# Seven products instead of eight for one more row pair in three stages of a two-layer decoder kernel

## The chip, the cores and the metric

The kernel runs on one core of one Trainium2 chip. The metric is the device time of one execution in microseconds (us). Three runs of the kernel before took 2260.9, 2261.01 and 2262.21 us, median 2261.01.

## The reference

The reference is a trunk of two decoder layers in float32 over 256 tokens of width 2048. Layer 0 mixes tokens with a gated linear recurrence (HGRN2, 12 heads of 128), layer 1 with gated linear attention (GLA, 4 heads, key width 192, value width 384). In both, one input projection also feeds a cross-attention of four heads into 256 memory tokens, and a SwiGLU feed-forward network follows. Cut to what the change touches:

```
# layer 0
q, f, i, g, xq = split(hn @ w_in)          # MIX_WIDTH = 1536 columns each, xq 512
f = sigmoid(f);  k = 1 - f;  q = silu(q)   # with a learned lower bound for f
o = chunked_linear_attention(q, k, i, log f)
y = rmsnorm_per_head(o) * silu(g)
# layer 1
q, k, v, g, gk_low, xq = split(hn @ w_in)  # q and k 768 columns, v and g 1536
# both
h = h + concat(y, memory_attention(xq)) @ w_out
```

`hn` is the normalized `h`; the kernel multiplies the row scales in after the projection.

## The kernel before

**Products.** All float32 products run on TensorE as three matmuls each: both factors are split into a high part (rounded to fp32r by ScalarE) and a low part (the rest, by VectorE), and a product is high x high, high x low and low x high. Activations are the stationary factor (128 rows of `h` turned, times 128 tokens), weights the moving one (512 columns, 384 in layer 1).

**Row pairs.** `project_two` (line 528 on) computes two column blocks of a weight matrix at once, for two tiles of 128 tokens, over the 2048 rows taken as eight pairs of 128-row slices. A pair is then a 2x2-by-2x2 block product. In a plan string with one letter per pair, `-` does it plainly, in eight products (24 matmuls, two `split` calls), and `S` in seven (21 matmuls) by a Strassen-like scheme (`seven`): it needs sums of the weight blocks (`raw` tiles, more subtractions on VectorE and four `split` calls) and sums of the activation blocks, which are made once per layer and kept (`Pair.more`, four extra factors in two parts). The letters S take pairs 0, 1, 2 ... in this order; the letters `-` take the pairs from the count of S on. Where `fed` holds (layer 0), one of the weight sums of an S is made by the load itself: SP loads one block, POOL's queue adds a second block onto it by an accumulating DMA.

**Buffers.** Three `raw` tiles hold loaded weights, six `parts` tiles the split ones; a plain pair takes two `parts`, an S pair three and one of two small `part` tiles. The memory keys and values that the attention reads also lie in `parts` buffers while it runs. The tag `tq` has eight buffers: a `more` takes one, a quad of turned mixer outputs (`y_0` to `y_3`) two.

**Layer 0, first mixer.** `h_quad` turns the normalized input (names `hx`); pairs below `SEVEN` get a `more`. Then come the xq projection (`hx`) and three groups of four heads. Each group g has two stages of `project_two`: forget gate and query (`hf0`, `hf1`, `hf2` in the trace), then value and output gate (`hv0`, `hv1`, `hv2`; with plan `----SSS-`, in the last group `----SS--`). After the last group comes the output projection: `wo` (512 columns, over the four y quads in the order 3, 0, 1, 2), then `wo0p`, and so on.

**Layer 1, second mixer.** Two pairs of heads; each has a key and query stage (`gk0`, `gk1`) and two value and gate stages (`gg00` to `gg11`, plan `-----SS-`). Here `fed` is off, and VectorE makes the sum.

**The queue of pieces.** The attention-like work between projections is cut into pieces and queued by `later`; `step` takes the next piece off the queue and issues it. A stage calls `step` twice in each plain pair (once for each 128-row slice), and once more where over `MANY` = 12 pieces wait; an S pair calls it only where over 12 wait. After each f/q stage 18 pieces are queued: two empty ones, `turn_f`, `turn_q`, two empty ones, and the twelve of `gated_scores` (`even_diagonal`, `pairs`, `level(2)` to `level(6)`, `across`, with empty ones between). After each value stage come `read` (readout, norm and gate) and `turn_y` (turning the result into a y quad) with empty ones before and between. In `wo` a step comes at five places, and ahead of the last y quad `y_done` issues all that is left (`flush`). The empty pieces space dependent pieces apart.

**Order.** Instructions are issued in the order of the program, but a list scheduler in the compiler puts a later instruction of an engine ahead of one that it expects not to be ready. Each engine then runs its list in order.

Of the kernel before, what the change touches and what calls it, by code (L numbers as in the profile page):

```python
# [13 lines left out]
AF = mybir.ActivationFunctionType  # L14
# [9 lines left out]
MIX = 1536  # L24
# [4 lines left out]
DK = 192  # L29
# [11 lines left out]
def trunk_kernel(ctx: ExitStack, tc: tile.TileContext, x, mem, norm_mix, norm_ffn, norm_mem,  # L41
# [210 lines left out]
    def later(*pieces):  # L252
        pending.extend(pieces)
# [391 lines left out]
        return ps  # L645


    SEVEN = 3
    MANY = 12


# [101 lines left out]
    for l in range(2):  # L753
# [6 lines left out]
        if l == 0:  # L760
# [4 lines left out]
            hq, ss, first_turns = {}, new_ss("ss_x"), []  # L765
# [207 lines left out]
    def hgrn_group(w, g, hq, r, yq):  # L973

        st = {}

        def stages(plan, *what):
            dst = []

            def give():  # L980
                for c0, name, func in what:
                    tag, bufs = ("stg", 2) if name in "fq" else (name, 1)
                    dst.append(work.tile([P, NT, 512], F32, tag=tag, name=f"{name}s{g}", bufs=bufs))
                return [lambda t, d=d: d[:, t, :] for d in dst]

            (ca, na, fa), (cb, nb, fb) = what
            project_two(hq["pairs"], plan, w, ca + 512 * g, cb + 512 * g, 512, f"h{na}{g}", give)
            for d, (c0, name, func) in zip(dst, what):
                for t in range(NT):
                    ac.activation(out=d[:, t, :], in_=d[:, t, :], func=func, scale=r[:, t:t + 1])  # L990
            return dst

        def turn_f():
            F = work.tile([P, NT, 4, P], F32, tag="F", name=f"F{g}")
            K = st["K"] = work.tile([P, NT, 4, P], F32, tag="K", name=f"K{g}")
            for j in range(2):
                tp = transposes([lambda t, c=2 * j + i: fs[:, t, c * P:(c + 1) * P] for i in range(2)], f"tf{g}{j}")
                for i in range(2):
                    c = 2 * j + i
                    ve.tensor_scalar(out=F[:, :, c, :], in0=tp[:, i * T:(i + 1) * T].rearrange("p (t c) -> p t c", c=P),  # L1000
                                            scalar1=oml[:, 4 * g + c:4 * g + c + 1],
                                            scalar2=lb[:, 4 * g + c:4 * g + c + 1], op0=ALU.mult, op1=ALU.add)
            ve.tensor_scalar(out=K, in0=F, scalar1=-1.0, scalar2=1.0, op0=ALU.mult, op1=ALU.add)
            first_keys(st, f"h{g}")
            decays(st, F, f"h{g}")

        def turn_q():
            Q = st["Q"] = work.tile([P, 2, NT, 4, P], F32, tag="Q", name=f"Q{g}")
            put_queries(st, Q, [by_tiles([lambda t, c=2 * j + i: qs[:, t, c * P:(c + 1) * P] for i in range(2)], f"tq{g}{j}")
                                for j in range(2)], 1.0)  # L1010

        def read():
            for t in range(NT):
                po = aux_ps(f"po{g}{t}")
                for a in range(4):
                    readout(st, a, 4, t, lambda s: v[:, s, a * P:(a + 1) * P], po[:, a * P:(a + 1) * P])
                ss = small.tile([P, 4], F32, tag="oss", name=f"oss{g}{t}")
                for a in range(4):
                    square_sum(po[:, a * P:(a + 1) * P], ss[:, a:a + 1], f"o{g}{t}{a}")
                ro = rstd(ss, 4, P, f"ro{g}{t}")  # L1020
                for a in range(4):
                    c = slice(a * P, (a + 1) * P)
                    ve.scalar_tensor_tensor(out=gate[:, t, c], in0=po[:, c], scalar=ro[:, a:a + 1],
                                                   in1=gate[:, t, c], op0=ALU.mult, op1=ALU.mult)

        def turn_y():
            yq[g] = make_quad(Quad("tq", f"y0_{g}"), lambda k, t: gate[:, t, k * P:(k + 1) * P], lambda k: g_ho, same=True, back=True)

        fs, qs = stages("----SSS-", (MIX, "f", AF.Sigmoid), (0, "q", AF.Silu))
        later(None, None, turn_f, turn_q, None, None, *gated_scores(st, [[0], [1], [2], [3]], f"h{g}"))  # L1030
        v, gate = stages("----SSS-" if g < 2 else "----SS--", (2 * MIX, "v", AF.Copy), (3 * MIX, "gate", AF.Silu))
        later(*([None, None, read, None, turn_y] if g < 2 else [read, None, turn_y]))
# [11 lines left out]
    def gla_pair(w, pr, dec, decay, hq, r, yq):  # L1044

        kw = MIX // 2
        st = {}

        def turn_k():
            decays(st, dec[pr], f"g{pr}")  # L1050
            K = st["K"] = work.tile([P, NT, 4, P], F32, tag="K", name=f"GK{pr}")
            for j in range(2):
                tp = by_tiles([lambda t, i=i: ks[:, t, j, i * P:(i + 1) * P] for i in range(2)], f"tgk{pr}{j}")
                ac.copy(out=K[:, :, 2 * j:2 * j + 2, :].rearrange("p t h c -> p t (h c)"), in_=tp.rearrange("p (t c) -> p t c", t=NT))
            first_keys(st, f"g{pr}")

        def turn_q():
            Q = st["Q"] = work.tile([P, 2, NT, 4, P], F32, tag="Q", name=f"GQ{pr}")
            put_queries(st, Q, [by_tiles([lambda t, i=i: qs[:, t, j, i * P:(i + 1) * P] for i in range(2)], f"tgq{pr}{j}")
                                for j in range(2)], float(DK) ** -0.5)  # L1060

        def read(a):
            hd = 2 * pr + a
            for t in range(NT):
                po = aux_ps(f"gpo{hd}{t}")
                readout(st, a, 2, t, lambda s: v[a][:, s, :], po[:, 0:DV])
                ss = small.tile([P, 4], F32, tag="oss", name=f"goss{hd}{t}")
                square_sum(po[:, 0:DV], ss[:, 0:1], f"go{hd}{t}")
                ro = rstd(ss[:, 0:1], 1, DV, f"gro{hd}{t}")
                ve.scalar_tensor_tensor(out=gate[a][:, t, :], in0=po[:, 0:DV], scalar=ro[:, 0:1],  # L1070
                                               in1=gate[a][:, t, :], op0=ALU.mult, op1=ALU.mult)

        def turn_y(a):
            hd = 2 * pr + a
            for i in range(3):
                f = 3 * hd + i
                q, k = divmod(f, 4)
                if k == 0:
                    yq[q] = Quad("tq", f"y1_{q}")
                tp = transposes([lambda t: gate[a][:, t, i * P:(i + 1) * P]], f"ty1_{f}", True)  # L1080
                yq[q].put(k, 1, tp[:, 0:T], g_go[:, i:i + 1])

        dst = []

        def give():
            for name in "kq":
                dst.append(work.tile([P, NT, 2, T], F32, tag="stg", name=f"gs{name}{pr}", bufs=2))
                nc.gpsimd.memset(dst[-1][:, :, :, DK:T], 0.0)
            return [lambda t, d=d: d[:, t, :, 0:DK] for d in dst]

        project_two(hq["pairs"], ("------S-", "------S-")[pr], w, kw + pr * 2 * DK, pr * 2 * DK, 2 * DK, f"gk{pr}", give,
                    lambda ps: ps.rearrange("p (a c) -> p a c", c=DK), fed=False)
        for d in dst:
            for t in range(NT):
                ac.activation(out=d[:, t, :, 0:DK], in_=d[:, t, :, 0:DK], func=AF.Copy, scale=r[:, t:t + 1])
        ks, qs = dst
        scores = gated_scores(st, [[0, 1], [2, 3]], f"g{pr}")
        if pr == 0:
            scores[5:5] = [lambda: decay(1), None]
        later(None, None, turn_k, turn_q, None, None, *scores)  # L1100
        GLA = (("-----SS-", "-----SS-"), ("-----SS-", "-----SS-"))
        gate, v = [], []
        for a in range(2):
            def give():
                for dst, tag in ((gate, "gate"), (v, "v")):
                    dst.append(work.tile([P, NT, DV], F32, tag=tag, name=f"g{tag}{pr}{a}"))
                return [lambda t, d=d[a]: d[:, t, :] for d in (gate, v)]

            project_two(hq["pairs"], GLA[pr][a], w, 2 * kw + MIX + (2 * pr + a) * DV, 2 * kw + (2 * pr + a) * DV, DV,
                        f"gg{pr}{a}", give, fed=False)  # L1110
            for dst, func in ((gate[a], AF.Silu), (v[a], AF.Copy)):
                for t in range(NT):
                    ac.activation(out=dst[:, t, :], in_=dst[:, t, :], func=func, scale=r[:, t:t + 1])
            later(None, None, lambda a=a: read(a), None, lambda a=a: turn_y(a))
# [170 lines left out]
    for l in range(2):  # L1285
# [33 lines left out]
        if l == 0:  # L1319
            hq = {}  # L1320
# [81 lines left out]
```

## Time and profile before

One profiled execution took 2261.07 us by the device clock; its span from first to last instruction is 2259.0 us, so 2.07 us lie around it.

| | of the span |
|---|---|
| TensorE matmul (PE) busy | 2245.2 us, 10710 instructions |
| TensorE weight load (PEld) busy | 1903.1 us |
| VectorE (DVE) busy | 1974.4 us |
| ScalarE (ACT) busy | 1425.3 us |
| GpSimd (POOL) busy | 202.3 us |
| HBM read | 468.45 MB |
| granted TensorE clock, mean | 0.999 |

In the rows of the timeline the first number is the start in us from the span's start, the second the length of one entry (merged entries have a count, x12), then engine, line, operation and `out<-in`. A bracket gives the idle time of the engine before the entry and what ended it. Nearly all instructions have line 151, the helper that issues them, so tile names tell them apart: `hf1p` is the accumulator of stage hf1, `parts34d` the fourth split tile of weight load 34, `raw` a loaded weight block, `slh` a score level, `pxh` the piece `across`, `po` the readout in `read`, `tp_y_2h` the turning in `turn_y`, `gates` the output gate. Weight loads 20 to 27 belong to hf0, 28 to 35 to hv0, 36 to 43 to hf1, 44 to 51 to hv1.

### The profile page before, as it was taken

The numbers are of one execution on the slowest core, as the hardware profiler recorded it, in microseconds if no ns is written. First come the engines' busy times: TensorE is split into PE (matmuls) and PEld (weight loads), VectorE is DVE, ScalarE is ACT, GpSimd is POOL, SyncE is SP. The second block draws the span as 40 slices with busy tenths as digits, with TensorE's granted clock in tenths as the row PEclk, the third lists the DMA queues.
The fourth block names the chain that finished last, engine by engine and source line by source line (L and its number), as shares of the span: only waits on it lengthen the run. The fifth ranks groups of instructions, "written<-read, shape, count | busy, mean of one in ns | idle before, by whom it ended". The sixth has DMA issues, their size and how long they took to land.

```text
span 2259.0 us, 30203 instructions
## 1 busy us (share of the span) xinstructions
PE 2245.2 (99%) x10710; PEld 1903.1 (84%) x10710; DVE 1974.4 (87%) x2459; ACT 1425.3 (63%) x1938; POOL 202.3 (9%) x205
## 2 busy tenths in 40 slices
PE   9999999999999999999999999999999999999998
PEld 7888888888888888888889999988888888888887
DVE  6889899898898989988986887889889898888987
ACT  7656656565666666665665665566566666666664
POOL 1000100000111111111100000000011111111110
PEclk9999999999999999999999999999999999999999
DMA  8656655665676777777765455566677777777774
GB/s 295 215 169 212 203 182 171 196 196 182 210 241 213 244 234 216 228 233 227 232 216 171 137 165 182 166 205 200 201 230 226 227 232 222 230 228 220 240 235 155
DMA packets 255691, 473.60 MB, mean 210 GB/s; under 512 B 17807, under 2 KB 47283, under 8 KB 255283
## 3 DMA queue, kind: packets, MB, share of 16 engines
q1 hardware_dynamic: 233507, 429.65, 56.8%
q0 software_dynamic: 20736, 37.76, 10.5%
q10 hardware_dynamic: 1296, 4.26, 0.5%
q8 instruction: 84, 1.38, 0.2%
q14 instruction: 68, 0.56, 0.1%
HBM read 468.45 MB, written 3.15 MB: 209 GB/s over the span
## 4 chain that ended last, share of the span: by engine, by line
PE 94%; DVE 2%; issue 1%; DMA 1%; ACT 0%; SPq 0%; POOLq 0%; DVEq 0%; POOL 0%; ACTq 0%
PE f_p L151 37%; PE fd L151 17%; PE wo L151 4%; PE m1p L151 2%; PE hv2p L151 2%; PE hv1p L151 2%; PE hv0p L151 2%; PE hf0p L151 2%; PE wo0p L151 2%; PE wo1p L151 2%; PE hf2p L151 2%; PE hf1p L151 2%; PE m0p L151 2%; PE gk0p L151 1%; PE gk1p L151 1%; PE gg11p L151 1%
## 5 line engine op out<-in xcount | busy, mean ns | idle before, releaser
L151 DVE TENSOR_TENSOR raw<-raw 128x512 f32<-128x512 f32 (+3 forms) x330 | 303.7, 921 | 49.8 <-DMA raw<-in_w_gate_up_dram 30.9
L151 ACT CAST parts<-raw 128x1024 fp32r<-128x1024 f32 (+1 forms) x216 | 212.2, 1017 | 48.5 <-PE gx L151 6.3
L151 DVE TENSOR_TENSOR parts<-raw,parts 128x1024 fp32r<-128x1024 f32 (+1 forms) x196 | 223.9, 1176 | 20.2 <-ACT parts L151 20.0
L424 POOL DMA_DIRECT2D raw<-in_w_gate_up_dram x114 | 98.8, 867 | 960.9 <-DMA raw<-in_w_gate_up_dram 348.6
L151 ACT COPY h<-fd 128x512 f32<-128x512 f32 x80 | 46.2, 588 | 84.6 <-PE fd L151 81.7
L292 POOL TENSOR_TENSOR parts<-raw,parts 128x1024 fp32r<-128x1024 f32 x20 | 48.7, 2433 | 232.6 <-ACT parts L151 219.0
L151 ACT ACTIVATE s<-s,rf_r 128x512 f32<-128x512 f32 x44 | 31.8, 723 | 44.0 <-DVE s L151 43.9
L151 DVE TENSOR_TENSOR e<-f_p,e 128x512 f32<-128x512 f32 x66 | 45.1, 684 | 2.3
L151 ACT COPY fd<-h 128x512 f32<-128x512 f32 x82 | 45.3, 585 | 0.0
L151 PE MATMUL fd<-parts,s_0h 128*128 128x512 f32 x128 | 39.8, 392 | 0.0
L151 PE MATMUL fd<-parts,s_8h 128*128 128x512 f32 x128 | 39.8, 392 | 0.0
L151 PE MATMUL fd<-parts,s_6h 128*128 128x512 f32 x128 | 39.8, 392 | 0.0
L151 PE MATMUL fd<-parts,s_4h 128*128 128x512 f32 x128 | 39.8, 392 | 0.0
L151 PE MATMUL fd<-parts,s_2h 128*128 128x512 f32 x128 | 39.8, 392 | 0.0
L151 PE MATMUL fd<-parts,s_5h 128*128 128x512 f32 x128 | 39.4, 389 | 0.0
L151 PE MATMUL fd<-parts,s_1h 128*128 128x512 f32 x128 | 39.4, 389 | 0.0
L151 PE MATMUL fd<-parts,s_7h 128*128 128x512 f32 x128 | 39.4, 389 | 0.0
L151 PE MATMUL fd<-parts,s_3h 128*128 128x512 f32 x128 | 39.4, 389 | 0.0
L151 DVE TENSOR_TENSOR s<-f_p,e 128x512 f32<-128x512 f32 x44 | 30.3, 688 | 10.0 <-PE f_p L151 8.1
L424 POOL DMA_DIRECT2D raw<-in_hgrn_w_in_dram x17 | 14.8, 874 | 210.8 <-DMA raw<-in_hgrn_w_in_dram 125.6
L151 DVE SCALAR_TENSOR_TENSOR s<-e,rf_r,s 128x512 f32<-128x512 f32 x44 | 31.0, 745 | 0.2
L151 PEld LDWEIGHTS fd<-parts,s_1h 128*128 128x128 f32 x128 | 24.0, 188 | 5.0
(5728 smaller groups left out, 7298.9 us busy)
## 6 DMA issues: line engine op xcount, KB each, us to landing
raw<-in_w_gate_up_dram SPq DMA_DIRECT2D x238, 512.0 KB, 4.8
raw<-in_w_down_dram SPq DMA_DIRECT2D x80, 1024.0 KB, 5.9
raw<-in_w_gate_up_dram SPq DMA_DIRECT2D x228, 256.0 KB, 4.0
raw<-in_hgrn_w_in_dram SPq DMA_DIRECT2D x79, 512.0 KB, 4.8
raw<-in_gla_w_in_dram SPq DMA_DIRECT2D x96, 384.0 KB, 3.9
raw<-in_w_gate_up_dram POOLq DMA_DIRECT2D x114, 256.0 KB, 5.3
raw<-in_w_out_dram SPq DMA_DIRECT2D x16, 1024.0 KB, 5.4
raw<-in_w_mem_kv_dram SPq DMA_DIRECT2D x27, 512.0 KB, 5.5
```

What stands on the lines that cost most here:

```text
L151: ins = func(*args, **kwargs)
L292: low = (nc.gpsimd if free_port else ve).tensor_tensor(out=both[:, 1, k:j, 0:m], in0=src[:, k:j, :], in1=both[:, 0, k:j, 0:m].bitcast(F32) ...
L424: nc.gpsimd.dma_start(out=raw[:, 1, 0:n], in_=rows[1], accum_op=ALU.add)
```

## The change

`SEVEN` goes from 3 to 4, so pair 3 of the first mixer's input also gets its extra factors. The f/q plan of all three groups goes from `----SSS-` to `---SSSS-`: pair 3 is done in seven products instead of eight, and four plain pairs are left instead of five. In both key and query stages of the second mixer the plan goes from `------S-` to `-----SS-`: pair 1, whose extra factors are there already, is done in seven products too. The value stages keep their plans.

```
-    SEVEN = 3
+    SEVEN = 4
...
-        fs, qs = stages("----SSS-", (MIX, "f", AF.Sigmoid), (0, "q", AF.Silu))
+        fs, qs = stages("---SSSS-", (MIX, "f", AF.Sigmoid), (0, "q", AF.Silu))
...
-        project_two(hq["pairs"], ("------S-", "------S-")[pr], w, kw + pr * 2 * DK, pr * 2 * DK, 2 * DK, f"gk{pr}", give,
+        project_two(hq["pairs"], "-----SS-", w, kw + pr * 2 * DK, pr * 2 * DK, 2 * DK, f"gk{pr}", give,
                     lambda ps: ps.rearrange("p (a c) -> p a c", c=DK), fed=False)
```

## The prediction

> **What bounds the kernel now.** I read the page first, for the share of each engine and the chain that ended last.
>
> ```profile
> span 2259.0 us, 30203 instructions
> PE 2245.2 (99%) x10710; PEld 1903.1 (84%) x10710; DVE 1974.4 (87%) x2459; ACT 1425.3 (63%) x1938; POOL 202.3 (9%) x205
> ...
> PE 94%; DVE 2%; issue 1%; DMA 1%; ACT 0%; SPq 0%; POOLq 0%; DVEq 0%; POOL 0%; ACTq 0%
> ```
>
> TensorE is busy for all but 13.8 us of the span, and the chain of waits runs through it. So a matmul that goes is time gained, as long as the engines that feed TensorE keep up. The table of busy time by stretch shows where that is close. The rows are hf0, hv0, hf1, hv1, then gk0 and gk1.
>
> ```profile
> core 0: us, PE busy (x) PEld busy (x) DVE busy (x) ACT busy (x) POOL busy (x), PEclk, DMA share, GB/s
> 126.30:177.60 51.30, 51.30 (x240) 43.03 (x241) 43.84 (x61) 29.33 (x45) 3.60 (x4) 1.00 0.61 181
> 177.60:225.50 47.90, 47.90 (x242) 40.46 (x241) 46.63 (x67) 29.02 (x37) 2.59 (x3) 1.00 0.64 190
> 225.50:271.50 46.00, 46.00 (x237) 39.21 (x236) 40.52 (x57) 27.20 (x46) 5.53 (x6) 1.00 0.62 185
> 274.20:322.50 48.30, 48.29 (x242) 40.34 (x241) 48.00 (x70) 30.39 (x38) 2.65 (x3) 1.00 0.62 188
> 1233.80:1277.60 43.80, 43.80 (x253) 42.67 (x252) 33.57 (x58) 28.20 (x48) 1.09 (x3) 1.00 0.43 138
> 1359.00:1394.40 35.40, 35.40 (x203) 34.57 (x203) 24.66 (x37) 19.25 (x31) 1.55 (x3) 1.00 0.57 179
> ```
>
> TensorE has no gap in any of them. VectorE has 7.5 us free in hf0 and 5.5 us in hf1, but 1.3 and 0.3 us in the value stages hv0 and hv1, and over 10 us in gk0 and gk1. The change adds VectorE work to stages that have room, next to stages that have none.
>
> **The matmuls that go.** The timeline of TensorE in hf0 shows the last S pair and the plain pair behind it; two rows of gk0 follow.
>
> ```profile
> 167.25 0.84 PE L151 MATMUL hf0p<-parts26a,hx2x 128*128 128x512 f32 x3
> ...
> 172.01 2.88 PE L151 MATMUL hf0p<-parts27a,hx7x 128*128 128x512 f32 x12
> 174.73 2.88 PE L151 MATMUL hf0p<-parts27b,hx7x 128*128 128x512 f32 x12
> ...
> 1273.26 2.24 PE L151 MATMUL gk0p<-parts231a,hm_7x 128*128 128x384 f32 x12
> 1275.34 2.24 PE L151 MATMUL gk0p<-parts231b,hm_7x 128*128 128x384 f32 x12
> ```
>
> Twelve matmuls take 174.73 - 172.01 = 2.72 us, so one is 0.227 us; the S pair takes 172.01 - 167.25 = 4.76 us, which is 21 of them. An S saves three: 0.68 us in layer 0, and by 1275.34 - 1273.26 = 2.08 us for twelve, 0.52 us in layer 1. Three stages and two stages: 3 x 0.68 + 2 x 0.52 = **3.08 us gained**, 15 matmuls of 10710.
>
> **The weight sums that come.** VectorE's timeline in hf0 has one whole S pair and one plain pair.
>
> ```profile
> 160.43 1.23 DVE L151 TENSOR_TENSOR parts26b<-raw,parts26b 128x1024 fp32r<-128x1024 f32 x1
> ...
> 166.58 1.22 DVE L151 TENSOR_TENSOR parts27a<-raw,parts27a 128x1024 fp32r<-128x1024 f32 x1
> ...
> 168.85 1.22 DVE L151 TENSOR_TENSOR parts28a<-raw,parts28a 128x1024 fp32r<-128x1024 f32 x1
> ```
>
> From 160.43 to 166.58 is one S (6.15 us), from there to 168.85 one plain pair (2.27 us): VectorE gets 3.9 us more per swapped pair. An S outlasts its own 4.76 us on TensorE, so in a run of S pairs VectorE loses its lead. How much lead is left is the distance between the last split of the last S and its first use, here for hf0, hv0 and hv1 (VectorE's row, then TensorE's):
>
> ```profile
> 165.44 1.23 DVE L151 TENSOR_TENSOR parts26d<-raw,parts26d 128x1024 fp32r<-128x1024 f32 x1
> 169.29 0.84 PE L151 MATMUL hf0p<-parts26d,hx2m 128*128 128x512 f32 x3
> ...
> 213.85 1.23 DVE L151 TENSOR_TENSOR parts34d<-raw,parts34d 128x1024 fp32r<-128x1024 f32 x1
> 216.28 0.84 PE L151 MATMUL hv0p<-parts34d,hx2m 128*128 128x512 f32 x3
> ...
> 310.86 1.23 DVE L151 TENSOR_TENSOR parts50d<-raw,parts50d 128x1024 fp32r<-128x1024 f32 x1
> 313.24 0.84 PE L151 MATMUL hv1p<-parts50d,hx2m 128*128 128x512 f32 x3
> ```
>
> The split ends 2.6 us early in hf0 (169.29 - 166.67), 1.2 in hv0, 1.15 in hv1. Were none of the new work covered, each group would come 3.9 + 0.68 = 4.6 us late against TensorE, and hv0 and hv1 would each stall for 4.6 - 1.2 = 3.4 us; hv2 has only two S, and I give it nothing. What covers it is VectorE's free time in hf0 and hf1. Much of it is of this kind (ScalarE's row, then VectorE's):
>
> ```profile
> 151.79 1.05 ACT L151 CAST parts25b<-raw 128x1024 fp32r<-128x1024 f32 x1 [2.56 <-PE hf0p L151]
> 152.87 1.23 DVE L151 TENSOR_TENSOR parts25b<-raw,parts25b 128x1024 fp32r<-128x1024 f32 x1 [1.49 <-ACT parts25b L151]
> ```
>
> ScalarE waits for TensorE to give back a `parts` buffer, VectorE for ScalarE. An S that starts one pair earlier can use that. In hf0 7.5 us free against 4.6 us: covered. In hf1 part of the 5.5 us is not of that kind:
>
> ```profile
> 252.34 1.13 DVE L151 SCALAR_TENSOR_TENSOR gates<-po,ro_r,gates 128x128 f32<-128x128 f32 x4 [1.15 <-POOL ro_r L189]
> 254.66 1.13 DVE L151 SCALAR_TENSOR_TENSOR gates<-po,ro_r,gates 128x128 f32<-128x128 f32 x4 [1.12 <-POOL ro_r L189]
> ```
>
> These 2.3 us are waits for POOL inside `read`, and they move with it (below). 5.5 - 2.3 = 3.2 us plus the lead of 1.15 against 4.6 leaves 0.2 us uncovered if all of it can be used, 1.8 if half. I take **0.8 us lost** in hv1; bounds 0 and 2 x 3.4 = 6.8.
>
> ScalarE gets the same kind of work with 29.3 of 51.3 us busy: nothing. In gk0 and gk1 an unfed S adds one more VectorE sum of 384 columns; 3.9 us and one operation against 10 free: nothing, at most 1 us in gk0, where the attention's buffers are still held.
>
> **Loads.** An S in layer 0 is loaded by three SP issues and one on POOL in place of two on SP, and moves 256 KB more.
>
> ```profile
> raw<-in_hgrn_w_in_dram POOLq DMA_DIRECT2D x17, 256.0 KB, 4.3
> ```
>
> Seventeen become twenty. DMA is at 0.61 to 0.64 in these stages, and the new load is issued when a `raw` tile comes free, a pair earlier than it is needed. Behind POOL's issue stands only the small power operation of `read`, which comes several pairs later. Nothing; in layer 1 the issues stay two.
>
> **The extra factors of pair 3** are made once, while `hx` runs.
>
> ```profile
> 117.13 0.69 DVE L151 TENSOR_TENSOR hx2m<-hx2g,hx2m 128x512 fp32r<-128x512 f32 x1
> 117.73 0.48 DVE L151 SCALAR_TENSOR_TENSOR hx3x<-tp_hx,pv,hx3x 128x256 fp32r<-128x256 f32 x1
> ...
> 123.19 2.88 PE L151 MATMUL hx<-parts,hx3x 128*128 128x512 f32 x12
> ```
>
> They cost two operations like the first, some small ones, and two copies on ScalarE, less than 3 us; pair 3's plain factors are ready 5.0 us (123.19 - 118.21) before TensorE wants them. Nothing. A fourth `more` fills `tq` (4 + 2 + 2 = 8); `y_1` takes the two that hf2 has freed, since its `turn_y` now comes after hf2.
>
> **The pieces that move.** This is the term that decides. A plain pair gives two steps; an f/q stage had ten and has eight. In group 0 exactly eight pieces of the cross-attention wait, so all fit, the last two at the end of hf0. After hv0 ten pieces wait in both programs (five of group 0's scores, then two empty, `read`, empty, `turn_y`). hf1 took all ten; with eight steps it leaves an empty one and `turn_y` for hv1. Counting on, with the extra step while over 12 wait, hf2 leaves `read`, an empty one and `turn_y`, and hv2 ends with eight pieces in place of six: `level(4)`, `level(5)`, empty, `level(6)`, `across`, `read`, empty, `turn_y`. The five steps of `wo` take the first five, and `y_done` has to issue `read` and `turn_y` together, just ahead of the last y quad. Before, `read` was the fourth step of `wo`, with a whole quad of matmuls behind it:
>
> ```profile
> 430.85 1.05 PE L151 MATMUL pxh<-Q,K 128*128 128x128 f32 x8
> 434.47 1.05 PE L151 MATMUL po<-vs,sch 128*128 128x128 f32 x8
> ...
> 437.07 0.71 PE L151 MATMUL wo<-parts,y_1h 128*128 128x512 f32 x2
> ...
> 442.61 0.27 PE L151 MATMUL tp_y_2h<-ident,gates 128*128 128x128 f32 x1
> 444.50 1.19 PE L151 MATMUL wo<-parts,y_2h 128*128 128x512 f32 x4 [0.85 <-ACT y_2h L151]
> 445.53 0.85 PE L151 MATMUL wo0p<-parts72a,y_2h 128*128 128x512 f32 x3
> ```
>
> `read` starts at 434.47, TensorE's part of it ends at 437.07, then 5.5 us of matmuls on `y_1` run, and the turning starts at 442.61 without a wait. VectorE's last gating shows how long the chain behind `read` really is (sums of squares on ScalarE, the power on POOL, twice):
>
> ```profile
> 441.05 1.13 DVE L151 SCALAR_TENSOR_TENSOR gates<-po,ro_r,gates 128x128 f32<-128x128 f32 x4 [1.19 <-POOL ro_r L189]
> ```
>
> It ends at 442.18, 7.7 us after `read` started; the first turns need only half of these four, so 7.3 us. Of these TensorE works 2.6. With the matmuls on `y_1` already done, it has nothing for 7.3 - 2.6 = **4.7 us lost**. The row at 445.53 shows that the scheduler fills such gaps with later products, but those too read `y_2`, and the six `parts` are all held by loads that want it (two for the rest of `wo`, four for the first two pairs of `wo0p`). Bounds: 0 if something fills it, 5.1 if the turning waits for all four.
>
> **Sum.** 2261.07 - 3.08 + 0.8 + 4.7 = 2263.5 us; the profiled execution is 0.06 above the median, so I leave that.
>
> **Rivals.**
> *The gap is filled.* If the scheduler has other matmuls for it, or the chain runs as the pieces of TensorE allow, only the gain and VectorE's 0 to 0.8 us stay: 2261.07 - 3.08 = 2258.0 to 2258.8. For it: TensorE is kept without a gap everywhere in the table. Against it: the buffers above. Chance 0.2.
> *VectorE becomes the bound in the value stages.* If its waits in hf0 and hf1 are not usable, hv0 and hv1 each stall 3.4 us: 2261.07 - 3.08 + 6.8 + 4.7 = 2269.5, slower by 0.37%. It decides once the lead of 1.2 us at the third S of a value stage is gone. For it: 46.6 of 47.9 us busy. Against: the free time just ahead. Chance 0.13.
> *TensorE comes back slow from the gap.* Every stretch of the table has a granted clock of 1.00, and none has a gap near 4.7 us. If the clock halved after it, the 24 matmuls on `y_2` (5.44 us) would take up to as long again; half of that is 2.7 us: 2266.2. Chance 0.12. [...]
>
> **How the numbers follow.** My own case has chance 0.5 (2261.5 to 2265.5), the rivals 0.45, 0.05 is left for a schedule that I don't foresee. Predicted: 2263.5 us. The range from 2257.3 to 2268.5 reaches over the filled gap below and half of VectorE's rival above. A change of 0.2% (4.5 us) is about what can be told from none. No sum falls more than 4.5 below: faster 0.04. My case and the filled gap lie within; VectorE's case, part of the slow clock and the upper edge of mine don't: same 0.7, slower 0.26.
>
> **What would show it.** TensorE's count falls to 10695. The chain in the first mixer has hf0 to hf2 each 0.7 us shorter by their own matmuls; `po` of hf1 comes at its last half pair, `slh` rows stand in `wo`; `po` and `tp_y_2h` follow each other with some 4.7 us of idle time, released by VectorE's `gates`, and the granted clock stays 1.00. The last split of hv1's third S is less than 1 us ahead of its use, or behind it. If `tp_y_2h` follows without a gap, the main term is wrong; if TensorE waits for `parts` in hv0, the cover is.

## The result, and the profile after

The changed kernel took 2270.39 us (median of five runs, 2268.66 to 2272.64) against 2262.21 us for the kernel before beside it (2260.9 to 2262.58): a ratio of 1.0040, 95% interval 1.0029 to 1.0052. It is slower by 0.4%, and the time lies outside the predicted range. A second run of the same kernel gave 2272.14 us and a ratio of 1.0046 (1.0033 to 1.0060).

The page of the changed kernel, with its shares and its chain:

```profile
span 2268.1 us, 30226 instructions
PE 2247.1 (99%) x10695; PEld 1902.5 (84%) x10695; DVE 1993.3 (88%) x2485; ACT 1435.0 (63%) x1950; POOL 204.8 (9%) x208
...
PE 91%; DVE 3%; ACT 2%; DMA 2%; issue 1%; POOL 0%; SPq 0%; POOLq 0%; DVEq 0%; ACTq 0%
```

TensorE has 15 matmuls fewer, as said, and yet counts as busy for 1.9 us longer. The idle time grows from 13.8 to 21.0 us, and the chain has lost 3 points of TensorE to VectorE, ScalarE and DMA. The table of busy time by stretch, for hf0, hv0, hf1, hv1, gk0 and gk1 (each from its first matmul to about that of the next stage):

```profile
126.80:180.00 53.20, 50.96 (x236) 42.10 (x236) 46.01 (x64) 29.00 (x45) 4.45 (x5) 1.00 0.62 183
180.00:229.00 49.00, 48.99 (x247) 41.12 (x246) 48.25 (x70) 31.98 (x41) 3.45 (x4) 1.00 0.62 189
229.00:275.30 46.30, 46.30 (x231) 39.27 (x231) 44.42 (x53) 27.86 (x45) 4.58 (x5) 1.00 0.72 217
275.30:326.50 51.20, 49.51 (x249) 41.20 (x248) 48.78 (x77) 31.65 (x41) 4.62 (x5) 1.00 0.55 167
1244.10:1287.60 43.50, 43.50 (x250) 42.20 (x249) 33.86 (x59) 28.45 (x50) 1.09 (x3) 1.00 0.44 140
1368.80:1403.60 34.80, 34.80 (x200) 33.97 (x199) 27.72 (x42) 19.84 (x32) 2.15 (x3) 1.00 0.57 181
```

In hf0 TensorE now idles for 2.2 us, in hv1 for 1.7; before, neither stage had a gap. gk0 and gk1 are shorter by half a microsecond and still without a gap.

Since pieces move over the borders of the stages, the account has to be made over a stretch that holds them all. The next table has the time from the first matmul of one stage to the first of the next, read off TensorE's timeline; the last row is the first mixer from hf0 to the feed-forward network (us):

| stage | before | after | difference |
|---|---|---|---|
| hf0 | 51.02 | 53.17 | +2.15 |
| hv0 | 48.71 | 49.05 | +0.34 |
| hf1 and hv1 | 96.96 | 97.48 | +0.52 |
| hf2 and hv2 | 98.66 | 99.44 | +0.78 |
| wo to the end of the output projection | 94.49 | 101.44 | +6.95 |
| **hf0 to the feed-forward network** | 389.84 | 400.58 | **+10.74** |
| gk0, gk1 | 79.38 | 78.39 | -0.99 |

The rest of the span, which no edit touches, differs by -0.7 us, so the span is 9.1 us longer. I use the stretch from hf0 to the feed-forward network below, because the untouched parts vary between profiled executions: the stage `m0p` near the start, which is the same in all kernels here, lasted 49.15 us in the kernel before and 50.62 us in one of the experiments. The stretch itself repeats better. In the second run of the changed kernel it took 400.33 us (hf0 52.46, hv1 51.51, hv2 52.82, from wo on 101.15), and in an experiment that leaves the first mixer as it was (`gla_only`) 390.42 against 389.84. So each stretch below is one execution, and differences of half a microsecond mean nothing.

**The end of group 2's mixer.** TensorE's timeline of the changed kernel in `wo`:

```profile
445.93 1.05 PE L151 MATMUL po<-vs,sch 128*128 128x128 f32 x8
...
448.38 0.39 PE L151 MATMUL po<-vs,sch 128*128 128x128 f32 x2
450.56 0.30 PE L151 MATMUL tp_y_2h<-ident,gates 128*128 128x128 f32 x1 [1.79 <-DVE gates L151]
451.08 0.30 PE L151 MATMUL tp_y_2h<-ident,gates 128*128 128x128 f32 x1 [0.22 <-DVE gates L151]
452.86 0.33 PE L151 MATMUL tp_y_2h<-turned_id,gates 128*128 128x128 f32 x1 [1.48 <-DVE gates L151]
...
454.22 2.07 PE L151 MATMUL wo<-parts,y_2h 128*128 128x512 f32 x4 [0.26 <-ACT y_2h L151]
```

`read` and `turn_y` stand together ahead of the last y quad, with three idle stretches released by VectorE's `gates` and one by the copy. From the first `po` to the first product on `y_2` it takes 454.22 - 445.93 = 8.29 us. Before, it took 444.50 - 434.47 = 10.03 us with 24 matmuls on `y_1` inside, 5.45 us at 0.227 each. So 8.29 - 4.58 = 3.7 us are lost here. And then there are the rows behind the gap, in the table by stretch:

```profile
451.00:454.20 3.20, 1.40 (x7) 0.82 (x7) 1.39 (x6) 0.72 (x2) 1.93 (x2) 0.95 0.64 231
454.20:457.60 3.40, 3.38 (x9) 2.67 (x10) 3.40 (x9) 1.58 (x3) 0.00 (x0) 0.54 0.48 77
457.60:461.20 3.60, 3.60 (x17) 3.00 (x16) 2.04 (x6) 1.57 (x2) 0.00 (x0) 1.00 0.00 0
```

The granted clock (the column ahead of the last two) falls to 0.54 for 3.4 us. Cut where it changes, it is 1.00 from 450.50 to 453.91, 0.50 from there to 457.32 and 1.00 again to 460.73: 3.41 us at half clock. Matmuls take longer there: the first four on `y_2` take 2.07 us, where the kernel before had 1.19.

**The waits between.** TensorE's waits from the start of hf0 to the start of wo, in the changed kernel; the kernel before has one line in this stretch, the wait of `tx` for `xs`.

```profile
PE ap L151 <- DVE prob L151: 2.0, 1, 2.0
PE tp_y_1h L151 <- DVE gates L151: 1.9, 2, 1.2
PE tp_y_0h L151 <- DVE gates L151: 1.1, 1, 1.1
PE slh L151 <- DVE Q L151: 0.6, 1, 0.6
PE hf0p L151 <- DVE parts26d L151: 0.3, 1, 0.3
```

Three of the five (four waits) belong to the pieces of groups 0 and 1, two to hf0. None is a wait for `parts` in a value stage.

**The wait in hf0.** `ap` belongs to the cross-attention and waits for `prob`, which VectorE scales. VectorE's own timeline shows why that is late:

```profile
134.46 0.69 DVE L151 TENSOR_TENSOR raw<-raw 128x512 f32<-128x512 f32 x1 [3.43 <-DMA raw<-in_hgrn_w_in_dram]
```

This is the first weight sum of hf0's first S pair, and VectorE stands 3.43 us for its load. The chain of waits around it has these pieces (start, duration, what):

```profile
123.42 2.77 DMA raw<-in_hgrn_w_in_dram
126.19 0.03 POOLq L424
...
126.80 7.56 DMA raw<-in_hgrn_w_in_dram
```

SP's block lands first, then POOL issues the block that is added to it, and that takes 7.56 us to land. In this time the DMA engines are busy at 0.96 (mean of 126.80 to 134.40), with three more loads that SP issued from 126.29 on. In the kernel before, the same operation waited for 0.36 us:

```profile
133.47 0.69 DVE L151 TENSOR_TENSOR raw<-raw 128x512 f32<-128x512 f32 x1 [0.36 <-DMA raw<-in_hgrn_w_in_dram]
```

There POOL had issued the block at 129.22, 4.25 us ahead of the operation, and the DMA engines were busy at 0.65 (mean of 129.22 to 133.47).

### The profile page after: what moved, and what is told of

Read it like the earlier page. It is cut to its first block, busy times and chain, and to the rows that moved or that the text cites. A ratio compares the mean times of both kernels' runs of the same rounds, so it can differ in the third digit from the quotient of the medians.

```text
span 2268.1 us, 30226 instructions
## 1 busy us (share of the span) xinstructions
PE 2247.1 (99%) x10695; PEld 1902.5 (84%) x10695; DVE 1993.3 (88%) x2485; ACT 1435.0 (63%) x1950; POOL 204.8 (9%) x208
## 4 chain that ended last, share of the span: by engine, by line
PE 91%; DVE 3%; ACT 2%; DMA 2%; issue 1%; POOL 0%; SPq 0%; POOLq 0%; DVEq 0%; ACTq 0%
PE f_p L151 39%; PE fd L151 19%; PE wo L151 4%; PE m1p L151 2%; PE hv0p L151 2%; PE wo1p L151 2%; PE wo0p L151 2%; PE fd_0p L151 2%; PE hf1p L151 2%; PE hv2p L151 1%; PE gg11p L151 1%; PE gg01p L151 1%; PE gg10p L151 1%; PE gk1p L151 1%; PE gg00p L151 1%
## 5 line engine op out<-in xcount | busy, mean ns | idle before, releaser
L151 DVE TENSOR_TENSOR raw<-raw 128x512 f32<-128x512 f32 (+3 forms) x342 | 313.7, 918 | 33.7 <-DMA raw<-in_w_gate_up_dram 17.0
```

The source lines that it names most:

```text
L151: ins = func(*args, **kwargs)
```

## The experiments

All ratios are against the kernel before, run beside the experiment on the same chip. "The stretch" is the one of the table above, hf0 to the feed-forward network, 389.84 us before and 400.58 after.

### Each half of the change alone

The second mixer's plan alone, on the kernel before (`gla_only`):

```
-        project_two(hq["pairs"], ("------S-", "------S-")[pr], w, ...
+        project_two(hq["pairs"], "-----SS-", w, ...
```

> Only the second mixer's plans are changed. Theory A (the second mixer's part is free of side effects): six matmuls of 0.17 us go, and between the start of gx and the start of wo1p TensorE is 1.0 us shorter than before; the whole comes out 1.0 us faster, about 2260. Rival (its second S loads VectorE too): no change or up to 1 us slower.

Measured: 2260.73 us against 2261.31, ratio 0.9995 (0.9986 to 1.0004). gk0 takes 43.59 us against 44.00 and gk1 34.87 against 35.39: 0.93 us gained, by matmuls that are not there, with nothing lost around them. The gain is too small for the runs to tell from nothing, but the stages show it.

The other half without its products: all products as before, but the fourth plain pair of the f/q stages issues no piece, so that the pieces come where the changed kernel has them (`steps_only`):

```
             for k, (lf, rt) in enumerate(((b00, b01), (b10, b11))):
-                step()
+                if not (name[:2] == "hf" and at == 3):
+                    step()
```

> The kernel before, but the fourth plain pair of each f/q stage calls no step, so the queue's pieces stand where the changed kernel has them, and all products stay as before. Theory A (the moved pieces are what costs): the gap before y_2 of some 3.7 us, the slow clock behind it of 1.5 us and the waits for gates in hv1 and hv2 of 3 us are all there; 6 to 9 us slower than before, about 2269. Rival B (the heavier load on VectorE from the fourth S costs most): under 2 us slower.

Measured: 2270.26 us, ratio 1.0038 (1.0023 to 1.0053), no less than the whole change. Its stretch is 396.72 us, 6.88 longer than before; 6.71 of that lies behind the start of wo. The same three waits stand ahead of `y_2`, and the same slow clock behind them:

```profile
447.85 0.30 PE L151 MATMUL tp_y_2h<-ident,gates 128*128 128x128 f32 x1 [1.79 <-DVE gates L151]
448.36 0.30 PE L151 MATMUL tp_y_2h<-ident,gates 128*128 128x128 f32 x1 [0.22 <-DVE gates L151]
450.14 0.33 PE L151 MATMUL tp_y_2h<-turned_id,gates 128*128 128x128 f32 x1 [1.48 <-DVE gates L151]
```

```profile
448.00:451.50 3.50, 1.80 (x8) 0.98 (x7) 1.68 (x7) 0.69 (x1) 1.01 (x1) 0.87 0.69 225
451.50:454.90 3.40, 3.40 (x11) 2.72 (x11) 3.33 (x8) 1.81 (x3) 0.92 (x1) 0.63 0.38 83
```

So the place of the pieces, with no S pair added, makes a kernel that is slower by 0.4%, as the first theory had it (though the waits for `gates` in hv1 and hv2 come to 1.2 us here and not 3). But its rival is not gone. The extra S pairs save 2.04 us of matmuls, and the changed kernel's stretch is still 3.86 us longer than this one: they cost 5.9 us in other ways. By stage, with 0.68 us put back for each S, that is 2.8 us in hf0, 0.3 in hv0, nothing in hf1 and hf2, 1.2 in hv1 (51.17 against 50.01), 1.3 in hv2 (52.42 against 51.08) and 0.2 from wo on. The runs themselves don't show it (2270.26 and 2270.39): the gain in gk0 and gk1 and the untouched parts, 2.3 us longer in this one execution, hide it.

### The clock behind the gap

The changed kernel with 16 matmuls of 512 columns between `read` and `turn_y` of the last group. They are additional work on `y_3`, and their result is read by nobody (`warm_gap`):

```
+        def warm():
+            spare = bank("warm")
+            for i in range(16):
+                pe.matmul(spare, yq[3].h[:, 0, 0:P], yq[3].h[:, 0:2, :].rearrange("p k t -> p (k t)"), start=True, stop=True)
+
         def y_done():
+            if l == 0:
+                pending[1] = warm
             flush()
```

> The changed kernel, with sixteen matmuls of 512 columns whose result nobody reads put between read and turn_y of the last group, to keep TensorE busy through the gap before y_2. If the idle stretch is what halves the clock, the granted clock stays 1.00 behind it and the 24 matmuls on y_2 take 5.5 us again in place of 7.0: 1.4 us faster than the changed kernel, about 2268.5. Rival (the clock drops for another reason, or the fillers come in the way): the clock dips all the same, no gain or up to 1 us slower.

Measured: 2269.68 us, ratio 1.0034 (1.0021 to 1.0047). The timeline and the table by stretch:

```profile
448.56 3.89 PE L151 MATMUL warm<-y_3h 128*128 128x512 f32 x16
452.29 0.27 PE L151 MATMUL tp_y_2h<-ident,gates 128*128 128x128 f32 x1
...
454.26 1.20 PE L151 MATMUL wo<-parts,y_2h 128*128 128x512 f32 x4 [0.26 <-ACT y_2h L151]
```

```profile
454.20:460.00 5.80, 5.74 (x25) 4.78 (x26) 5.63 (x13) 3.19 (x6) 0.89 (x1) 1.00 0.31 55
```

The products on `y_2` start where they started (454.26), four of them take 1.20 us again, and from the start of wo to the feed-forward network it is 100.01 us in place of 101.44. So the slow clock costs 1.43 us here, and with the idle time filled the clock stays at 1.00. What it costs differs between executions: from the first product on `y_2` to the feed-forward network it is 71.77 us in this kernel and 71.78 in the kernel before, but 73.20, 72.63 and 72.95 in the two runs of the changed kernel and in `steps_only`, so 0.9 to 1.4 us. The runs alone can't tell 0.7 us (2269.68 against 2270.39); the stage and the clock column can.

### The pieces put back

First by two steps inside the first S pair of each f/q stage of the changed kernel, so that a stage has ten again (`steps_kept`):

```
-                for b in (1, 6, 7, 5, 2, 4, 3) if last else (3, 2, 1, 6, 7, 5, 4):
+                for j, b in enumerate((1, 6, 7, 5, 2, 4, 3) if last else (3, 2, 1, 6, 7, 5, 4)):
+                    if name[:2] == "hf" and at == 3 and j in (0, 4):
+                        step()
```

> The changed kernel, but the first S of each f/q stage calls step twice like the plain pair that it replaced, so that all pieces stand where the kernel before has them. Theory A (moved pieces): no gap before y_2, no wait for gates, clock 1.00; what stays is the 2 us wait in hf0 that follows VectorE's 3.4 us wait for the early load of the first S; 2261.5 - 3.1 + 2 to 2.5 = about 2261. Rival B (VectorE's load): still 2266 or more.

Measured: 2269.7 us, ratio 1.0034 (1.0021 to 1.0046). From wo on it takes 94.49 us, as before the change, so all 6.95 us there do come from the moved pieces. But hf0 takes 55.18 us, hf1 52.07 and hf2 50.21, against 51.02, 47.88 and 47.89 before, and the stretch is 401.30 us, the longest of all. So the first theory, which had 2261, missed the time, and the time alone would fit its rival (2266 or more). TensorE's longest waits in this kernel from hf0 to the feed-forward network, beside that of `y_2h`:

```profile
PE hf1p L151 <- DVE gates L151: 3.1, 1, 3.1
PE ap L151 <- DVE prob L151: 2.7, 2, 2.5
PE hf2p L151 <- DVE gates L151: 2.4, 2, 2.0
```

Products of the projection itself wait for VectorE's gating, whose result they don't read. What they share with `read` is PSUM: by the code an S opens the accumulators of seven blocks, and `read` holds two tiles of the same memory until the gating has read them. That this is the cause was argued from the code and not tried by itself. In hf0 the wait is for `prob` (2.54 us), and the granted clock behind it is lower: 0.79 from 145 to 150 us, 0.87 from 150 to 155. Both ways of `read` are thus bad: behind the S pairs it is too late for `wo`, among them it stands in their way.

Then by leaving out two empty pieces instead of adding steps (`two_empties`):

```
-        later(*([None, None, read, None, turn_y] if g < 2 else [read, None, turn_y]))
+        later(read, None, turn_y)
```

> The changed kernel without the two empty pieces ahead of read in groups 0 and 1, so that the eight pieces that hf1 and hf2 find fit their eight steps, read stands in the last plain half pair before the S run, turn_y in the last pair of the stage, and the last group's read in wo a quad ahead of turn_y, all as before. Theory A (the queue): no gap before y_2, no wait for gates in hv1 and hv2, clock 1.00 throughout; left is hf0 with its 2 us: about 2260.5. Rival B (the S runs load VectorE): stalls of 1 to 3 us in each of hv0, hv1 and hv2 stay, 2264 or more. Rival C (read ahead of a run of four S is short of PSUM banks, which an S pair all needs): TensorE waits 2 to 3 us on gates in hf1 and hf2, 2264 to 2266.

Measured: 2264.98 us, ratio 1.0015 (1.0006 to 1.0024). From wo on it takes 94.47 us, and the mean granted clock of the profiled run is 0.999, as in the kernel before: of the loss of 0.4%, 0.25 points are gone with two placeholders that do no work. But the first theory, with only hf0 left (2260.5), misses by 4.5 us. hv1 and hv2 stay 1.1 and 0.7 us longer than before (50.16 and 51.51 against 49.08 and 50.77), though all pieces are back: stalls in the value stages as in rival B, but smaller, and there the longest wait is for ScalarE's `fs`; what makes that late is open. And hf2 waits 1.1 us for `gates`, as in rival C. These waits are left (beside that of `y_2h`, 0.8 us, which the kernel before has too, and two of 0.3 us and less):

```profile
PE ap L151 <- DVE prob L151: 1.7, 1, 1.7
PE tf L151 <- ACT fs L151: 1.4, 2, 1.1
PE hf2p L151 <- DVE gates L151: 1.1, 1, 1.1
```

### The added load

The same kernel, with the first S of hf0 loaded without the adding DMA, so that VectorE makes that sum too (`two_empties_unfed`):

```
+        stage_fed = fed
         for at, (p, kind) in enumerate(zip(order, plan)):
+            fed = stage_fed and not (name == "hf0" and at == 3)
```

> As two_empties, and the first S of hf0 is loaded without the accumulating DMA; VectorE makes that one sum itself (0.6 us). Theory A (VectorE's 3.4 us wait at the start of hf0 is the late landing of this load, and TensorE's 2.0 us wait for the softmax follows from it): that wait is gone, hf0 is 1.5 to 2.2 us shorter than in two_empties, about 2258.5. Rival (the softmax is late because VectorE has more splits in that stretch): hf0 as long as in two_empties or 0.5 us longer.

Measured: 2264.86 us, ratio 1.0012 (1.0003 to 1.0021). hf0 takes 51.29 us in place of 52.87, so the late load costs 1.58 us there, and VectorE is better off with one operation more than with the wait. (The edit also takes 256 KB of loading away; whether the adding or the amount makes the load late was not separated.) The wait for `prob` is off the list; what is left, again beside that of `y_2h`:

```profile
PE hf2p L151 <- DVE gates L151: 0.8, 1, 0.8
PE tf L151 <- ACT fs L151: 0.8, 1, 0.8
PE slh L151 <- DVE Th L151: 0.4, 1, 0.4
PE hf0p L151 <- DVE parts26d L151: 0.3, 1, 0.3
```

The runs of the two kernels don't show the gain (2264.98 and 2264.86 us, where the theory had 2258.5); the stage does, and it does again in the next pair of kernels. In the stretch this kernel is at 392.88 us, still 3.0 above the kernel before, 0.75 of it in hv1 and 1.0 in hv2.

### Group 0 alone

In group 0 all the waiting pieces fit into hf0 with either plan, so an S pair there should move nothing. The changed kernel with hf1 and hf2 set back, with the added load and without it (`group0` and `group0_unfed`):

```
-        fs, qs = stages("---SSSS-", (MIX, "f", AF.Sigmoid), (0, "q", AF.Silu))
+        fs, qs = stages("---SSSS-" if g == 0 else "----SSS-", (MIX, "f", AF.Sigmoid), (0, "q", AF.Silu))
```

> The changed kernel, with hf1 and hf2 set back to three S pairs; group 0 and the second mixer keep theirs. Theory (the moved pieces cost nearly all; the fed load of hf0's first S costs 1.6 us more): group 0 has only eight pieces and all fit in hf0 in both programs, so wo takes 94.5 us as in the kernel before, no clock window, and hf1 to hv2 stand as before. Left are hf0 at 51.0 - 0.7 + 2.8 = 53.2 us, as in the changed kernel, and the second mixer's -1.0: some +1.1 us, ratio about 1.0005. Rival (the extra S pairs themselves cost, in whichever stage, through VectorE): hv0 and hv1 lose 1 us or more each against the kernel before, ratio 1.0015 or more.

> As group0, and the first S of hf0 is loaded without the accumulating DMA (VectorE makes its weight sum). Theory: hf0 goes back to some 51.3 us, TensorE waits no more for prob, so the time is 1.6 us below group0 and some 0.7 us below the kernel before: ratio 0.9995 to 1.0. Rival (the wait for prob is VectorE's own load and not the late DMA): hf0 stays at 53 us and the two runs agree.

Measured: 2263.49 us, ratio 1.0011 (1.0002 to 1.0019), and 2262.62 us, ratio 1.0002 (0.9993 to 1.0011). hf1 to the feed-forward network takes what it took before to within 0.03 us in each stage, so neither hv1 nor hv2 suffers from the S pair in hf0. hf0 takes 52.60 and 51.42 us, hv0 49.07 and 49.08 (before: 51.02 and 48.71). The wait for `prob` falls from 1.4 to 0.2 us. The same operation on VectorE, in the one and in the other kernel:

```profile
134.51 0.69 DVE L151 TENSOR_TENSOR raw<-raw 128x512 f32<-128x512 f32 x1 [2.91 <-DMA raw<-in_hgrn_w_in_dram]
```

```profile
135.63 0.69 DVE L151 TENSOR_TENSOR raw<-raw 128x512 f32<-128x512 f32 x1 [0.37 <-DMA raw<-in_hgrn_w_in_dram]
```

In the stretch the two kernels are 1.9 and 0.75 us longer than before; with the 0.9 to 1.0 us gained in gk0 and gk1 that is +0.9 and -0.2, where the theory gave +1.1 and -0.7. Both medians lie a microsecond higher, and the ratio of `group0_unfed` is above the range that the theory gave. The rival, which had hv0 and hv1 lose 1 us or more each, falls for the S pair of hf0: it is 0.36 us in hv0 and nothing in hv1. What the S pairs of hf1 and hf2 cost in hv1 and hv2 is not tested here, since these two are set back. But VectorE's load by itself does cost in hf0: of 52.60 - 51.02 + 0.68 = 2.26 us lost there, 1.18 go with the adding load, the rest stays (1.08). Some 0.4 of it stand at the split of `parts26d`, which VectorE finishes just behind its use. Even so, with the load mended and no piece moved, one S pair in hf0 saves 0.68 us of matmuls and leaves hf0 and hv0 0.77 us longer than before. No kernel tried here is measurably faster than the kernel before.

## Why the prediction was wrong

It named the largest cause and still missed the time: in the stretch it had -2.04 + 0.8 + 4.7 = +3.5 us, and it is +10.74. Term by term, for the changed kernel (us):

| step of the prediction | predicted | measured | from |
|---|---|---|---|
| The matmuls that go | -3.08 | -3.03 | 15 matmuls fewer; 0.99 of it read from gk0 and gk1 |
| The weight sums that come (hv1) | +0.8 | +0.7 | no wait for `parts` in hv1; instead about 0.4 in hf0 and 0.34 in hv0; more of it stands in the row of groups 0 and 1 |
| Loads | 0 | +2.0 | the wait of `ap` in hf0 (1.26 in the second run); 1.2 to 1.6 by experiment |
| The extra factors of pair 3 | 0 | 0 | hx to hf0: 25.60 against 25.57 |
| The pieces that move, last group | +4.7 | +3.7 | rows ahead of `y_2` |
| The same, groups 0 and 1 | not priced | +3.6 | four waits for `gates` and `Q`; without the S pairs (`steps_only`) 1.2 |
| TensorE comes back slow (a rival) | 0 | +1.43 | `warm_gap` |

Without the second mixer's part the measured rows add up to +9.4 us against the +10.74 of the stretch; 1.3 us stay without a name.

**The matmuls that go** was right, and so was the judgement that gk0 and gk1 have room for it.

**The pieces that move** failed in two ways. The counting was right: `read` and `turn_y` came together ahead of the last y quad, with more `slh` rows in wo, as foretold. For the last group the size was 1.0 us too high. Half of that is the turning, which is not one block behind the gating: two of its matmuls went early, in the wait for the second half, so that only 454.22 - 452.86 = 1.36 us of it lie behind the last wait for `gates` and not 1.9. The other half is the chain, which let the turning go on 452.86 - 445.93 = 6.9 us behind the start of `read` and not 7.3. But I priced the move in the last group only. In groups 0 and 1 I had worked out that `turn_y` goes to the next stage, and gave that no price and no reason. That stage has matmuls in plenty, but the turning stands in TensorE's list where it was expected to be ready, and where it wasn't, TensorE took nothing from behind it: it stood for 1.09, 1.15 and 0.72 us.

```profile
278.10 0.33 PE L151 MATMUL tp_y_0h<-turned_id,gates 128*128 128x128 f32 x1 [1.09 <-DVE gates L151]
...
382.23 0.33 PE L151 MATMUL tp_y_1h<-ident,gates 128*128 128x128 f32 x1 [1.15 <-DVE gates L151]
...
386.15 0.33 PE L151 MATMUL tp_y_1h<-turned_id,gates 128*128 128x128 f32 x1 [0.72 <-DVE gates L151]
```

Around these rows are products of hv1 and hv2 that could have run: the two behind the wait at 382.23 read the same tiles (`parts61a`, `hx3x`) as the eight ahead of it. In `steps_only` the same three waits are 0.38, 0.57 and 0.29 us, so with the S pairs and their VectorE work they are two to three times as long; this is part of the 5.9 us that the S pairs cost.

**Loads: "Nothing"** is a step that failed outright. It rested on the share of DMA and on the load being issued a pair ahead of its use. The trace of before had the number against it in its own issues: an added block takes 4.3 us to land behind a first block that must have landed, and VectorE comes to the first S a pair earlier. Here it took 7.56 us, at a time when SP's own loads are under way, and VectorE stood ready at 134.46 - 3.43 = 131.03. That does not stall TensorE by the product of the S but by what is queued behind the sum on VectorE, the scaling of `prob`. I had asked what stands behind POOL's issue, and not what stands behind VectorE's sum.

**The weight sums that come** failed as well. hv1 does not stall for `parts`, and hf0, which I had called covered, and hv0 lose about 0.7 us. But the extra S pairs also delay what waits for VectorE's `gates`: against `steps_only`, where the pieces move in the same way, hv1 loses 1.2 us and hv2, to which I gave nothing, 1.3. The rival in which VectorE becomes the bound of the value stages gives nearly the measured time (2269.5 us), but by two stalls of 3.4 us in hv0 and hv1 that aren't there; a smaller form of it is. The lead did shrink to nothing, as these rows of hv1 show (VectorE's split of `parts50d`, then its first use):

```profile
314.43 1.22 DVE L151 TENSOR_TENSOR parts50d<-raw,parts50d 128x1024 fp32r<-128x1024 f32 x1 [0.24 <-ACT parts50d L151]
```

```profile
315.66 0.85 PE L151 MATMUL hv1p<-parts50d,hx2m 128*128 128x512 f32 x3
```

Before, the split ended 1.15 us ahead of that use; now it ends as the use begins. There is nothing left for any more VectorE work in that stage.

**The rival of the slow clock** came true, with 0.9 to 1.4 us in place of the 2.7 that its sum took. Those 2.7 us were my estimate, half of the 5.44 us of matmuls on `y_2`, without a run that had such a gap; the runs showed half clock for 3.4 us behind it, in the changed kernel and in `steps_only`. I gave the rival 0.12, and held it apart from my own case although its condition, an idle gap of some 4 us, was my own case.

Together: the sign and the main place were foreseen, the chance of "slower" was put too low at 0.26, and the range ended 1.9 us below the median, since three further costs (the load in hf0, the waits of groups 0 and 1, the slow clock) were taken as nothing or as a case by itself.

## What to carry to other kernels

Where pieces of another chain ride on the steps of a stage, a cheaper stage carries fewer of them; count what each piece lands behind, and price every place to which one moves, not only the last. A late operand stalled what was queued behind its reader (TensorE by 1.15 us ahead of `tp_y_1h` in hv2), and other work in the same stage covered nothing where it stood behind the wait. When a step of a prediction creates an idle gap on TensorE, the clock behind that gap belongs to the same sum: here it cost 0.9 to 1.4 us.

## What the runs showed of the hardware

The clock was halved behind less idle time than the 4.7 us that I had priced. The longest single wait ahead of `y_2` is 1.79 us; with the two lone turnings in between, TensorE was busy for 0.64 of the 4.10 us from 448.80 to 452.90. In `steps_kept` the clock fell behind one wait of 3.06 us in hf1, in the midst of dense products:

```profile
260.68 1.65 PE L151 MATMUL hf1p<-parts39c,hx0m 128*128 128x512 f32 x3 [3.06 <-DVE gates L151]
```

The table by stretch, three rows around this wait in `steps_kept`, then three around the gap of the changed kernel:

```profile
256.00:260.00 4.00, 1.62 (x8) 1.00 (x6) 3.07 (x7) 3.78 (x18) 1.61 (x2) 1.00 0.88 239
260.00:264.00 4.00, 3.32 (x8) 2.64 (x9) 3.10 (x10) 1.52 (x3) 1.91 (x1) 0.57 0.19 70
264.00:268.00 4.00, 4.00 (x20) 3.28 (x19) 4.00 (x5) 1.42 (x2) 0.00 (x0) 1.00 0.19 30
...
450.50:453.91 3.41, 1.65 (x8) 0.95 (x8) 1.89 (x8) 0.43 (x1) 1.93 (x2) 1.00 0.69 237
453.91:457.32 3.41, 3.15 (x8) 2.48 (x8) 3.12 (x7) 1.87 (x4) 0.00 (x0) 0.50 0.48 77
457.32:460.73 3.41, 3.41 (x16) 2.81 (x15) 1.85 (x6) 1.57 (x2) 0.00 (x0) 1.00 0.00 0
```

In the changed kernel 0.50 lasts 3.41 us. Counted as time at 0.50, the other slow stretches are as long: in `steps_kept` 2 x 0.43 x 4.00 = 3.4 us in hf1 and, behind the wait of 2.54 us in hf0, 2 x (0.21 + 0.13) x 5.00 = 3.4 us, and in `steps_only` 2 x (0.13 x 3.50 + 0.37 x 3.40) = 3.4 us. The wait of 1.96 us in hf0 of the changed kernel left the clock at 1.00 (first row of its table by stretch).

The longest single wait does not decide alone, then: 1.79 us ahead of `y_2` came before half clock, 1.96 us in hf0 did not. What separates the two, no run shows.
